# Splitting weight halves two halves ahead, and moving the form slots by 416 bytes

## The chip, the cores and the metric

The kernel runs on one NeuronCore of a Trainium2 chip. The metric is device time in microseconds (us). Three executions of the kernel before took 2930.47 us in the median (2928.84 to 2932.45).

The engines that matter here: TensorE (PE in the profile; its weight loads are listed as PEld), VectorE (DVE), ScalarE (ACT), GpSimd (POOL), and SyncE (SP), whose queue issues nearly all DMAs. Each engine runs its own instructions in the order in which the built program has them; semaphores make one engine wait for another. SBUF is the on-chip memory, with 128 partitions; an address below is a byte address within each partition. PSUM holds the results of matmuls in banks of 128x512 float32.

## The reference

One decoder layer in float32 for 512 tokens of width 2048. Two branches read the same normalised input: sliding-window attention and a gated delta rule over chunks of 64 tokens. Their outputs are gated, added, and projected once more.

```python
h = rms_norm(x, norm_w) * (1.0 + scale) + shift
proj = h @ w_in                      # 2048 x 21056
aq, ak, av, ag, d_qkv, dz, db, da, mg_a, mg_b = jnp.split(proj, ...)
a_out = swa_attention(aq, ak, av, sinks) * jax.nn.silu(ag)
y_a = a_out @ w_o_swa                # 2048 x 2048
d_qkv = causal_conv_silu(d_qkv, conv_w)
o = gated_delta_rule(dq, dk, dv, g, beta)
o = rms_norm(o, dn_norm_w) * jax.nn.silu(dz)
y_b = o @ w_o_dn                     # 4096 x 2048
y = jax.nn.sigmoid(mg_a) * y_a + jax.nn.sigmoid(mg_b) * y_b
return x + gate * (y @ w_out)        # 2048 x 2048
```

## The kernel before

**Products in three matmuls.** Weights and activations are float32, and each is split into a high part (a cast to the type fp32r) and a low part (the rest). A product is `wh*xh + wh*xl + wl*xh`, three matmuls (`mm3`, lines 265 to 267). `h` is kept split, as `hh` and `hl`. Weights come from DRAM in jobs of 1 MB (128x2048) and are split on the chip in halves of 128x1024: ACT casts (`whi`, line 68), DVE subtracts (`wlo`, line 69).

**Stages.** After the start-up (to about 120 us) come the delta rule's keys, attention, the delta rule's heads, and the closing chain (from about 1955 us). In the first three a job is one tile of 128 output channels (`channel_tile`): 16 pieces of the contraction, 8 in each half, three matmuls for each, so 24 matmuls in a half. The closing chain computes six 2048-wide products (the two gates `ga`, `gb`, the attention output, two halves of the delta output, the last projection) with a scheme of seven products for eight (`PRODUCTS`), on sums of quarters of the weights and of the activations. There a half holds 12 matmuls, and the activations are the stationary operand. The weight sums are made beside the earlier stages: `sums_of` loads quarters `q`, adds them on DVE (line 1490), and stores them to `s_d`. A solve (lines 819 and 827) runs on DVE beside the keys and the heads. In the heads a `scan` of four chunks runs for each of 16 groups; ACT and DVE copy and scale between its small matmuls (`vs`, line 972; `r`, line 960; `S`, lines 992 and 995).

**The weight line.** `jobs` lists all weights in the order of their use. Three counters run over it: `job_load` (loads written so far), `half_split` (halves split so far) and `half_used`. `half` hands out the half that a product needs, and splits it on the spot if that has not been written yet. When a product has been written with a half, `half_done` puts `split_half` on a list; at the next call of `pump` (after every second piece in a channel tile, after every half of tokens in the closing chain) `weight_tick` runs the list. `split_half` writes the cast and the subtraction of the next half, and after the second half of a job it puts `load_job` on the list for the pump after that, which writes the load of the job two later. So in the channel tiles, at the first pump of half n, the split of half n+1 is written.

**Buffers.** Raw weights have two buffers (`wraw`), and in the closing chain a third one (`oraw`, in the pool `braw`), which every third job uses from the 7th of the chain on; an extra `load_job` at the start of `tail` fills it first. Split halves have three buffers of `whi` and `wlo` (`whl`). A split needs its raw data landed and the third buffer free, that is, the product three halves before it done.

**Order.** The instructions are written by generators that `pump` steps beside the matmuls (`go`, `paced`, `beside`); `behind` ties an instruction to a place. A planner then settles each engine's order at build time: it runs the program with estimated durations, and an engine takes, of the instructions that are ready, the one written first. So the place in which an instruction is written is a priority, not a fixed position. DMAs on SP are ordered in the same way.

**Form slots.** The closing chain keeps the split activations in slots `f0` to `f8`, each a pair of 128x8x256 tiles of 8,192 bytes. Slots 5 to 8 take the place of `hh` and `hl` once these are done. Pools of the right side of SBUF are laid out downwards from its top: `work` (small tiles), `bf` (slots 2 to 4), `braw`, `bf01` (slots 0 and 1). In the built program `hh`, and later `f5h`, starts at 43,584, and all tiles of slots 5 to 8, `hh`, `hl`, `whi` and `wlo` start 64 bytes past a multiple of 512. The tiles of slots 0 to 4 start at 109,536 (`f0h`) to 191,456 (`f4l`), all of them 480 bytes past a multiple of 512. Between the end of `hl` (109,120) and `f0h` 416 bytes are unused.

Of the kernel before, what the change touches and what calls it, by code (L numbers as in the profile page):

```python
# [7 lines left out]
F32 = mybir.dt.float32  # L8
# [8 lines left out]
P = 128  # L17
# [35 lines left out]
class Layer:  # L53
# [148 lines left out]
    def load_job(self):  # L202
        j = self.job_load
        if j < len(self.jobs):
            src = self.jobs[j][1]
            third = j >= self.tail0 + 6 and (j - self.tail0) % 3 == 0
            pool, tag = (self.oraw, "rawo") if third else (self.wraw, "raw")
            raw = pool.tile([P, 2048], F32, tag=tag, name="raw")
            self.nc.sync.dma_start(out=raw[:, : src.shape[-1]], in_=src)
            self.raws[j] = raw  # L210
            self.job_load += 1
# [440 lines left out]
    def delta_keys(self):  # L652
        tc = self.tc
        dram = self.dram
        self.lt_d = dram.tile([2, 2, 16, 4, HD, HD], F32, name="lt_d")
        self.lab_d = dram.tile([VH, HD, 4, HD], F32, name="lab_d")
        self.ta_d = dram.tile([2, 16, 4, HD, HD], F32, name="ta_d")
        self.ts_d = dram.tile([2, 2, 16, 4, HD, HD], F32, name="ts_d")
        self.kT_d = dram.tile([KH, P, T], F32, name="kT_d")
        self.k_d = dram.tile([KH, P, T], F32, name="k_d")  # L660
        self.o_d = dram.tile([VH, P, T], F32, name="o_d")
        with ExitStack() as sa:
            self.ptp = sa.enter_context(tc.tile_pool(name="ptp", bufs=2, space=PSUM, reuse_waits="tile"))
            self.zpool = (sa.enter_context(tc.tile_pool(name="gwk", bufs=1, reuse_waits="tile")), "zth")
            wk = sa.enter_context(tc.tile_pool(name="dnA", bufs=2, reuse_waits="tile"))
            gp = sa.enter_context(tc.tile_pool(name="gates", bufs=1, reuse_waits="tile"))
            gates = self.gates(gp)
            self.go(gates, next(gates))
            gt = sa.enter_context(tc.tile_pool(name="gatew", bufs=1, reuse_waits="tile"))
            self.beside(self.gate(gt), 0.26, "gate")  # L670
            self.keys_done = []
            for g in range(NST):
                self.go(self.keys(wk, g, self.acc_k[g]), 10 + 8 * g)
            for h in ZAHEAD[:NFIRST]:
                self.z_tile(h)
            self.solved = []
            self.solves = self.paced(self.solve_all(), 0.36)
            ws = sa.enter_context(tc.tile_pool(name="wsumk", bufs=1, reuse_waits="tile"))
            sums = self.paced(self.weight_sums(ws, [0]), 1.7)
            for kind, j in self.mixed():  # L680
                if kind == "k":
                    self.go(self.keys(wk, j, self.channel_tile(f"k{j}")), 0)
                else:
                    self.z_tile(j)
            self.drain("gate")
            self.drain_slow(sums)
            self.drain_live()
# [391 lines left out]
    def tail(self, es, wk):  # L1079
# [4 lines left out]
        self.ys_d = self.dram.tile([5, P, 4, 256], F32, name="ys_d")  # L1084
        self.ya_d = self.dram.tile([4, 4, P, T], F32, name="ya_d")
        self.yo_d = self.dram.tile([4, 4, P, T], F32, name="yo_d")
        self.w = lambda name: wk.tile([P, T], F32, tag="w", name=name, bufs=2)
        self.ld = lambda name: wk.tile([P, T], F32, tag="ld", name=name, bufs=4)
        self.fo = lambda name: wk.tile([P, T], F32, tag="fo", name=name, bufs=4)
# [33 lines left out]
        for e, n, m in order:  # L1123
            name, form = PRODUCTS[m][:2]
# [757 lines left out]
```

## Time and profile before

| | before |
|---|---|
| median of 3 executions | 2930.47 us |
| the profiled execution, its own time | 2934.85 us |
| its span, from the first to the last instruction | 2933.1 us |
| mean granted clock of TensorE in it | 0.983 |
| PE busy | 2812.4 us (96%) |
| DVE busy | 2205.7 us (75%) |
| ACT busy | 1316.4 us (45%) |
| DMA, mean rate | 265 GB/s |

The profile is of one execution, taken by the hardware profiler. A row of waits reads: engine, tile and line that waited, what ended the wait, us in total, how often, the longest. A row of a group reads: line, engine, operation, out<-in, shapes, count, then busy us and mean ns of one, then idle us of the engine just before. Rows of stretches give the busy us of each engine with its instruction count, the granted clock of TensorE (1.00 is full speed), the busy share of the DMA engines and GB/s. Matmuls are pipelined: one is listed with about 0.39 us while the next starts 0.23 us after it.

### The profile page before, as it was taken

To read this page: it belongs to the slowest core of one execution; us is meant where nothing else is said; L and a number is where in the kernel's file an instruction comes from. 1 tells how busy PE (TensorE), PEld (TensorE's weight loads), DVE (VectorE), ACT (ScalarE), POOL (GpSimd) and SP (SyncE) were. 2 spreads that over 40 slices of the span, in tenths; PEclk is the share of its full clock that TensorE was granted. 3 is DMA by queue.
4 is the path that set the end of the run, shared out by engine and by line. 5 is a ranking of instruction groups with operands and counts; after the bars stand their busy time and mean duration, and the time that the engine had idled before them with its cause. 6 is when DMAs were issued, how large, how long until landed. Compare 5 with 4: busy or idle time off the path is not lost.

```text
span 2933.1 us, 38848 instructions
## 1 busy us (share of the span) xinstructions
PE 2812.4 (96%) x13864; PEld 2249.2 (77%) x13864; DVE 2205.7 (75%) x3422; ACT 1316.4 (45%) x2647; POOL 151.3 (5%) x124
## 2 busy tenths in 40 slices
PE   8999899899999999999997999999999999999999
PEld 6787677677776778878776777887878878778787
DVE  7876787778767768888865666768666878787876
ACT  5564433234454434344353434445444645444543
POOL 0001000000000001011000100100000000000000
PEclk9999999999999999999998999999999999999999
DMA  9889888464455548888868888866788989998875
GB/s 402 323 289 315 292 272 299 123 200 135 163 185 163 179 164 311 300 302 282 314 202 286 279 301 309 282 230 208 239 313 281 326 313 337 339 332 275 288 244 188
DMA packets 286565, 776.31 MB, mean 265 GB/s; under 512 B 82946, under 2 KB 107138, under 8 KB 241314
## 3 DMA queue, kind: packets, MB, share of 16 engines
q1 hardware_dynamic: 286372, 773.84, 76.7%
q8 instruction: 109, 1.79, 0.3%
q14 instruction: 84, 0.69, 0.1%
HBM read 588.84 MB, written 182.66 MB: 263 GB/s over the span
## 4 chain that ended last, share of the span: by engine, by line
PE 77%; DVE 10%; DMA 6%; ACT 3%; issue 3%; SPq 1%; POOL 0%; DVEq 0%; ACTq 0%; POOLq 0%
PE mm L267 13%; PE mm L265 13%; PE mm L266 13%; PE m L266 9%; PE m L267 9%; PE m L265 9%; DVE wlo L69 2%; DMA q<-in_w_q 1%; DMA s_d<-q 1%; DVE q L1490 1%; ACT whi L68 1%; PE pod L984 1%; PE pv L967 1%; PE O L1761 1%; PE pp L957 1%
## 5 line engine op out<-in xcount | busy, mean ns | idle before, releaser
L69 DVE TENSOR_TENSOR wlo<-raw,whi 128x1024 fp32r<-128x1024 f32 x588 | 722.7, 1235 | 327.8 <-ACT whi L68 326.2
L68 ACT CAST whi<-raw 128x1024 fp32r<-128x1024 f32 x588 | 612.4, 1050 | 697.6 <-PE m L267 400.2
L265 PE MATMUL mm<-hh,whi 128*128 128x512 f32 x2016 | 825.5, 409 | 24.7 <-ACT whi L68 24.3
L267 PE MATMUL mm<-hh,wlo 128*128 128x512 f32 x2016 | 803.9, 399 | 26.1 <-DVE wlo L69 26.0
L266 PE MATMUL mm<-hl,whi 128*128 128x512 f32 x2016 | 798.2, 396 | 0.0
L265 PEld LDWEIGHTS mm<-hh,whi 128*128 128x128 f32 x2016 | 384.4, 191 | 115.5 <-ACT whi L68 28.2
L267 PEld LDWEIGHTS mm<-hh,wlo 128*128 128x128 f32 x2016 | 383.6, 190 | 116.4 <-DVE wlo L69 34.4
L266 PEld LDWEIGHTS mm<-hl,whi 128*128 128x128 f32 x2016 | 384.4, 191 | 73.9 <-issue 1.5
L1490 DVE TENSOR_TENSOR q<-q,q 128x1024 f32<-128x1024 f32 (+1 forms) x224 | 244.3, 1091 | 16.3 <-DMA q<-in_w_q 14.9
L784 POOL TENSOR_SCALAR_AFFINE_SELECT E<-E 128x512 f32<-128x512 f32 x64 | 63.6, 1007 | 1048.1 <-DMA E<-g_rows 725.3
L827 DVE TENSOR_TENSOR A<-A,atmp 128x62 f32<-128x62 f32 (+30 forms) x124 | 110.0, 887 | 0.5
L819 DVE TENSOR_TENSOR atmp<-A 128x62 f32<-128x62 f32 (+30 forms) x124 | 108.6, 876 | 0.6
L642 DVE SCALAR_TENSOR_TENSOR yv<-mm,convh,yv 128x511 f32<-128x511 f32 (+2 forms) x96 | 71.4, 743 | 19.7 <-ACT yv L639 18.9
L790 ACT ACTIVATE E<-E,neg_g 128x128 f32<-128x128 f32 x256 | 79.2, 393 | 7.9 <-POOL E L784 7.8
L266 PE MATMUL m<-wlo,hh 128*128 128x512 f32 x192 | 76.9, 401 | 3.8 <-DVE wlo L69 3.8
L265 PE MATMUL m<-whi,hh 128*128 128x512 f32 x192 | 77.6, 406 | 2.0 <-ACT whi L68 1.8
L267 PE MATMUL m<-whi,hl 128*128 128x512 f32 x192 | 76.6, 400 | 0.0
L985 ACT COPY osb<-pod 128x256 f32<-128x256 f32 x64 | 23.8, 372 | 105.0 <-PE pod L984 80.2
L972 ACT ACTIVATE vs<-pv,kd 128x128 f32<-128x128 f32 x96 | 30.2, 365 | 81.0 <-PE pv L967 81.0
L266 PE MATMUL m<-wlo,f2h 128*128 128x512 f32 x160 | 63.7, 398 | 0.4 <-DVE wlo L69 0.4
L266 PE MATMUL m<-wlo,f0h 128*128 128x512 f32 x160 | 63.7, 398 | 0.0
L266 PE MATMUL m<-wlo,f3h 128*128 128x512 f32 x160 | 63.7, 398 | 0.0
(431 smaller groups left out, 4818.5 us busy)
## 6 DMA issues: line engine op xcount, KB each, us to landing
raw<-in_w_ch SPq DMA_DIRECT2D x126, 1024.0 KB
raw<-s_d SPq DMA_DIRECT2D x96, 1024.0 KB
q<-in_w_q SPq DMA_DIRECT2D x160, 512.0 KB
s_d<-q SPq DMA_DIRECT2D x160, 512.0 KB
raw<-in_w_q SPq DMA_DIRECT2D x72, 1024.0 KB
wa<-in_w_ada_ss SPq DMA_DIRECT2D x32, 1024.0 KB
gw<-in_w_ada_gate SPq DMA_DIRECT2D x16, 1024.0 KB
E<-g_rows SPq DMA_DIRECT2D x64, 256.0 KB
```

The costliest lines, as they stand in the source:

```text
L68: h = self.nc.scalar.copy(out=hi, in_=src)
L69: l = self.nc.vector.tensor_tensor(out=lo, in0=src, in1=hi.bitcast(F32), op=ALU.subtract)
L265: nc.tensor.matmul(ps, lhsT=wh, rhs=xh, start=first, stop=False)
L266: nc.tensor.matmul(ps, lhsT=wh, rhs=xl, start=False, stop=False)
L267: self.last_mm = nc.tensor.matmul(ps, lhsT=wl, rhs=xh, start=False, stop=last)
L642: nc.vector.scalar_tensor_tensor(out=y[:, s:], in0=ps[:, : T - s], scalar=w[:, j : j + 1], in1=y[:, s:], op0=ALU.mult, op1=ALU.add)
L784: self.last_mask = self.nc.gpsimd.affine_select(out=E, in_=E, pattern=[[0, NTB], [1, P]], compare_op=ALU.is_ge, fill=NEG, base=0, channel_ ...
L790: self.nc.scalar.activation(E[:, c, :], E[:, c, :], AF.Exp, bias=self.neg_g[:, c, h : h + 1])
L819: eng.tensor_tensor(out=t, in0=A[:, m : m + 1, m + 1 :].to_broadcast([P, m, n]), in1=A[:, :m, m : m + 1].to_broadcast([P, m, n]), op=ALU.mult,
L827: self.behind(eng.tensor_tensor(out=A[:, :m, m + 1 :], in0=A[:, :m, m + 1 :], in1=t, op=ALU.add))
L972: nc.scalar.activation(vs[:, e, :], pv[:, e, :], AF.Copy, scale=self.kd[:, c, 2 * g + e : 2 * g + e + 1])
L1490: self.behind(nc.vector.tensor_tensor(out=q[f], in0=q[x], in1=q[y], op=ALU.add))
```

## The change

Two splits more are put on the list once, at the start of the keys. Since every later split is put there by a `half_done`, the line of splits runs one half further ahead from then on: at the first pump of half n, the split of half n+2 is written, and each load of raw weights is written one half earlier too. The 7th load of the closing chain is then written in the heads, before the pool of the third raw buffer is opened; so the third buffer is used from the 10th job on. In the closing chain a tile of 104 float32 (416 bytes) is allocated first in the pool `work` and never used; what is allocated after it on the right side lies 416 bytes lower.

```diff
@@ load_job
-            third = j >= self.tail0 + 6 and (j - self.tail0) % 3 == 0
+            third = j >= self.tail0 + 9 and (j - self.tail0) % 3 == 0
             pool, tag = (self.oraw, "rawo") if third else (self.wraw, "raw")
@@ delta_keys
             self.beside(self.gate(gt), 0.26, "gate")
+            self.due += [self.split_half] * 2
             self.keys_done = []
@@ tail
         self.yo_d = self.dram.tile([4, 4, P, T], F32, name="yo_d")
+        wk.tile([P, 104], F32, name="align")
         self.w = lambda name: wk.tile([P, T], F32, tag="w", name=name, bufs=2)
```

## The prediction

> **What bounds the kernel now.** I read the shares of the engines first, then a table of five stages, then TensorE's waits stage by stage.
>
> ```profile
> span 2933.1 us, 38848 instructions
> PE 2812.4 (96%) x13864; PEld 2249.2 (77%) x13864; DVE 2205.7 (75%) x3422; ACT 1316.4 (45%) x2647; POOL 151.3 (5%) x124
> ...
> 120.00:550.00 430.00, 401.31 (x1845) 325.97 (x1843) 329.06 (x518) 185.05 (x463) 29.89 (x34) 0.97 0.84 281
> 550.00:1085.00 535.00, 524.31 (x2717) 396.07 (x2718) 411.96 (x833) 225.74 (x511) 34.03 (x22) 0.99 0.50 159
> 1085.00:1955.00 870.00, 825.08 (x4420) 673.87 (x4419) 647.91 (x993) 363.71 (x974) 87.18 (x64) 0.98 0.84 285
> 1955.00:2933.10 978.10, 956.77 (x4166) 774.36 (x4165) 722.16 (x940) 474.28 (x584) 0.00 (x0) 0.99 0.81 281
> ```
>
> TensorE is busy 2812.4 of 2933.1 us, so 121 us are idle; the stages are keys (from 120), attention (from 550), heads (from 1085) and closing chain (from 1955). The columns after the length are PE, PEld, DVE, ACT and POOL with their counts, then the granted clock, the DMA share and GB/s. No other engine is full in any stage: DVE is at 74 to 77%. So what counts is the idle time and the clock. The waits of TensorE, in the order keys, attention, heads, closing chain:
>
> ```profile
> PE mm L265 <- ACT whi L68: 9.2, 4, 5.0
> PE mm L267 <- DVE wlo L69: 7.0, 5, 3.7
> ...
> PE mm L267 <- DVE wlo L69: 2.9, 1, 2.9
> ...
> PE mm L267 <- DVE wlo L69: 16.2, 9, 6.0
> PE mm L265 <- ACT whi L68: 15.0, 9, 3.6
> PE pod L980 <- ACT vs L972: 5.2, 6, 1.7
> PE pp L957 <- DVE S L995: 3.0, 4, 1.9
> ...
> PE m L266 <- DVE wlo L69: 9.5, 7, 2.9
> PE m L265 <- ACT whi L68: 1.8, 1, 1.8
> ```
>
> Each row has the sum in us, the number, and the longest. Waits for a half of the weights make 9.2 + 7.0 + 2.9 + 16.2 + 15.0 = 50.3 us before 1955, and 11.3 us after it. None is over 6.0 us. A timeline around one of them, in the heads, shows why (columns: start, length, engine, line, operation, count, idle before):
>
> ```profile
> 1445.05 0.39 PE L266 MATMUL mm<-hl,whi 128*128 128x512 f32 x1
> 1449.64 0.80 PE L267 MATMUL mm<-hh,wlo 128*128 128x512 f32 x1 [4.20 <-DVE wlo L69]
> 1450.23 0.63 PE L265 MATMUL mm<-hh,whi 128*128 128x512 f32 x1
> ...
> 1443.39 1.98 ACT L68 CAST whi<-raw 128x1024 fp32r<-128x1024 f32 x2
> ...
> 1446.21 1.21 DVE L1490 TENSOR_TENSOR q<-q,q 128x1024 f32<-128x1024 f32 x1
> 1447.34 0.68 DVE L649 SCALAR_TENSOR_TENSOR yv<-th,yv 128x512 f32<-128x512 f32 x1
> 1447.95 0.50 DVE L819 TENSOR_TENSOR atmp<-A 128x342 f32<-128x342 f32 x1
> 1448.37 1.21 DVE L69 TENSOR_TENSOR wlo<-raw,whi 128x1024 fp32r<-128x1024 f32 x1
> ```
>
> The weights and their high part were there at 1445.4. The low part stood behind other work in DVE's order and came 4.2 us late, and after the stall the matmuls are 0.63 instead of 0.39 us long. The clock did that; here are the first, three of the middle and the sum of the 12 stretches of half clock that begin at such a wait between 120 and 1955:
>
> ```profile
> 277.43:280.84 3.41, 3.00 (x7) 2.42 (x8) 2.91 (x5) 3.17 (x11) 0.00 (x0) 0.50 0.96 197
> ...
> 1448.20:1455.02 6.82, 5.38 (x13) 3.85 (x14) 6.72 (x13) 0.63 (x1) 0.00 (x0) 0.50 0.98 338
> ...
> 1550.60:1564.25 13.65, 7.37 (x23) 5.88 (x24) 9.76 (x14) 4.09 (x11) 1.23 (x2) 0.50 0.78 277
> 1656.42:1659.82 3.40, 3.09 (x7) 2.50 (x8) 3.40 (x5) 0.52 (x2) 0.00 (x0) 0.50 0.00 0
> ...
> sum 64.75, PE 49.07 PEld 37.92 DVE 53.74 ACT 25.37 POOL 2.32; mean PE 4.09 PEld 3.16 DVE 4.48 ACT 2.11 POOL 0.19
> ```
>
> TensorE works 49.07 us in them at half speed, so half of that, 24.5 us, is lost. A wait for a half before 1955 thus costs half as much again: 50.3 + 24.5 = 74.8 us together.
>
> **Part one: the halves.** No instruction is added or removed; these two groups keep their counts.
>
> ```profile
> L69 DVE TENSOR_TENSOR wlo<-raw,whi 128x1024 fp32r<-128x1024 f32 x588 | 722.7, 1235 | 327.8 <-ACT whi L68 326.2
> L68 ACT CAST whi<-raw 128x1024 fp32r<-128x1024 f32 x588 | 612.4, 1050 | 697.6 <-PE m L267 400.2
> ```
>
> At the first pump of the keys two splits are written where there were none, 2 x 1.05 us on ACT and 2 x 1.24 on DVE; TensorE is then at half 16 with half 17 still to come, so nothing waits for them. From there on every split stands one half earlier in the written order. A half is 24 matmuls before 1955, at least 24 x 0.227 = 5.4 us (0.227 is 10.2/45 from the row of slot 8 below), and with other work between 870/110 = 7.9 us on average in the heads, which have 55 tiles of two halves. No wait is longer than that. So in the best case all 74.8 us go.
>
> Against that stand two things. First, the lateness is DVE's: from 1446.21 to 1449.6 it has no idle. Taken ahead, the subtraction makes everything that it passes 1.2 us later, and DVE is as far behind as before when TensorE comes to a product that cannot be prepared early: pod, pp, pv of the scan, which wait 5.2 + 3.0 us and some more now. Second, a half can be split only when its weights have landed, and only two raw buffers exist before 1955. The load of job j+2 is written at the pump after the second half of job j is split, so all loads move a half earlier too, past what SP issues in that time; SP already stands often at this place, for the subtraction that frees the buffer:
>
> ```profile
> SPq L209 <- DVE wlo L69: 593.5, 159, 11.6
> ...
> 583.76 0.38 SPq L209 DMA_DIRECT2D raw<-in_w_ch  x1
> ...
> 588.80 1.06 ACT L68 CAST whi<-raw 128x1024 fp32r<-128x1024 f32 x1 [3.14 <-DMA raw<-in_w_ch]
> ```
>
> A load alone takes 5.0 us (583.76 to 588.80), well inside the three halves that it has before and after. What it passes (stores s_d, loads q, E, qe, tt) is later once by one transfer, 5 us at most, since later loads pass no more than it did. DMA is at 84% in keys and heads, so the earlier place is worth something only if loads aren't already as late as the queue makes them. Bounds of the term: 0 and -74.8 us. I take 55%, -41 us: nearer the upper bound because every wait is shorter than the step, but not at it because DVE's lateness stays.
>
> In the closing chain the casts already run as early as a buffer allows:
>
> ```profile
> ACT whi L68 <- PE m L267: 370.2, 243, 3.4
> ...
> ACT whi L68 <- PE mm L266: 33.5, 12, 4.3
> ```
>
> From 2060 on 243 of some 300 casts wait for TensorE to let go of the third buffer (second row: in the heads 12 of 110). A place further ahead cannot make them earlier. Only the subtractions can win a place against other DVE work. Bounds 0 and -11.3; I take -3.
>
> **The third raw buffer** now starts with the 10th load of the chain instead of the 7th, as the 7th is written before that buffer exists. For three jobs the loads have two buffers: a job of two halves lasts 24 x 0.227 = 5.4 us there, and a buffer is held for the load (5.0) and two splits one half apart (2.7 + 1.05 + 1.24), 10.0 against 2 x 5.4. That fits; the cost is 0, and if a load is late by 2 us in each of the three, 6 us.
>
> **Part two: 416 bytes.** Slots 0 to 4 start at 480 bytes past a multiple of 512, slots 5 to 8 and both h tensors at 64 past one (given above). The tile of 416 bytes brings slots 0 to 4 to 64 as well. Their products differ today; 16 first matmuls of one product each:
>
> ```profile
> L265 PE MATMUL m<-whi,f8h x16: 389/389/389, 2895.0 to 2905.2; 128*128 128x512 f32 x16
> ...
> L265 PE MATMUL m<-whi,f3h x16: 394/394/394, 2905.9 to 2916.4; 128*128 128x512 f32 x16
> ...
> L265 PE MATMUL m<-whi,f0h 128*128 128x512 f32 x160 | 63.3, 396 | 0.0
> ...
> L265 PE MATMUL m<-whi,f4h 128*128 128x512 f32 x128 | 50.8, 398 | 0.0
> ```
>
> From the first to the 16th are 45 matmuls: 10.5 us for slot 3 and 10.2 for slot 8, so 0.3/45 = 6.7 ns each. Slots 0 to 3 have 160 such first matmuls each and slot 4 has 128: 768, times three is 2304 matmuls, times 6.7 ns is 15.4 us, all on TensorE, which is not waiting there. I take -15.4; the other bound is 0.
>
> [...] The rows show a difference between the two starts; I go by them.
>
> **Sum:** -41 - 3 + 0 - 15.4 = -59 against the profiled execution's 2934.85 us, which is 4.4 above the median of 2930.47: 2871 us by the median.
>
> **Rivals.** (a) All waits for halves go: -74.8 - 11.3 - 15.4, 2829 us. For it: no wait exceeds 6.0. Against it: DVE stays behind. (b) The two raw buffers are the limit: where a cast follows a landing, two ahead becomes one again, and only the slots and some 5 us remain: 2910. For it: 593.5 us of SP's waits and the 84%. Against it: at 1443 both halves were cast at once, so their data had been there. (c) The halves do as forecast, the slots' 6.7 ns come from something other than their start: 2886. (d) Slower: the cast now needs the buffer of the product that ends only as the position is reached; ACT and DVE stand at it, and the scan's copies vs and sums S queue behind, 1.05 + 1.24 us later. There are 48 such links (three in each of 16 groups), 110 us if all are hit, and TensorE waits for them. It turns the sign above 54% of the links (59/110); with three quarters hit, 2930 - 59 + 82 = 2953. Against it: in the heads only 12 of 110 casts wait for a buffer today, and the planner writes a split behind what is ready sooner. (e) No change by the noise: gains of (b) lost again in a new order, 2930.
>
> **How the numbers follow.** Forecast 0.42 (its own range 2850 to 2895), (a) 0.10, (b) 0.20, (c) 0.10, (d) 0.12, (e) 0.06. The range 2838 to 2932 leaves out most of (a) and (d). About 0.2% (6 us) is what a measurement can tell from no change: faster 0.82, same 0.06, slower 0.12.
>
> [...]
>
> **What would show it.** Right: the waits for whi and wlo before 1955 fall from 50 to under 20 us, stretches of half clock with them; slot 3 shows 389 ns and 10.2 us; the waits of pod, pp, pv and transposes rise a little. Wrong: casts ended by raw in number (b), slots still at 394 (c), or vs and S as TensorE's longest waits (d).

## The result

The changed kernel took 2912.14 us in the median of seven executions (2907.43 to 2922.3), the kernel before 2932.45 in the median of seven beside it. The ratio is 0.9935, with a 95% interval of 0.9919 to 0.9951: 19 us less, 14 to 24. The forecast was 2871, 59 less; its sign was right and its size was not.

**The profile after.** From the page, and from a table of three stretches: keys with attention, heads, closing chain. Here the borders are the first matmul of the heads' first tile and the first matmul of the chain, so that each kernel is cut at the same work. The columns are length, busy us of PE, PEld, DVE, ACT and POOL with their counts, granted clock, DMA share and GB/s. First the changed kernel:

```profile
span 2912.9 us, 38883 instructions
PE 2790.4 (96%) x13864; PEld 2243.9 (77%) x13864; DVE 2203.2 (76%) x3422; ACT 1319.0 (45%) x2647; POOL 158.2 (5%) x124
...
122.80:1090.90 968.10, 919.72 (x4540) 717.15 (x4539) 738.50 (x1345) 407.36 (x969) 62.93 (x56) 0.98 0.64 212
1090.90:1951.50 860.60, 822.94 (x4426) 672.54 (x4424) 644.98 (x990) 365.82 (x975) 95.05 (x64) 0.98 0.85 288
1951.50:2912.90 961.40, 939.52 (x4170) 772.44 (x4168) 722.77 (x944) 475.69 (x585) 0.00 (x0) 0.99 0.82 286
```

The kernel before, cut at the same matmuls:

```profile
122.90:1083.10 960.20, 920.82 (x4540) 718.10 (x4539) 737.85 (x1345) 406.97 (x969) 63.93 (x56) 0.98 0.65 214
1083.10:1954.30 871.20, 826.28 (x4426) 674.85 (x4424) 648.20 (x990) 364.48 (x975) 87.18 (x64) 0.98 0.84 285
1954.30:2933.10 978.80, 957.47 (x4171) 774.97 (x4168) 722.75 (x944) 474.98 (x585) 0.00 (x0) 0.99 0.81 281
```

The chain became 17.4 us shorter and the heads 10.6, but keys and attention 7.9 us longer. Up to the chain, where -41 was forecast, -2.8 remain (the start-up differs by 0.1). By these rows TensorE's idle time (length less PE) rose from 39.4 to 48.4 us in keys and attention and fell from 44.9 to 37.7 in the heads; its busy time fell by 4.4 us in the two together.

**The waits after.** TensorE's waits in the changed kernel, in the order keys, heads, closing chain (us in all, how often, the longest):

```profile
PE mm L267 <- DVE wlo L69: 9.4, 9, 2.4
PE mm L265 <- ACT whi L68: 6.4, 4, 2.6
PE pkk L757 <- ACT kT L750: 5.4, 7, 0.8
PE ptk L314 <- DVE y L649: 4.6, 1, 4.6
PE mm L265 <- DVE zth L307: 4.0, 2, 3.2
...
PE mm L267 <- DVE wlo L69: 12.2, 8, 2.8
PE mm L265 <- ACT whi L68: 7.8, 8, 1.8
PE pqk L919 <- DMA kT<-kT_d: 5.8, 1, 5.8
PE pto L314 <- DVE tt L936: 3.0, 3, 1.9
PE pv L968 <- DVE tt L936: 2.1, 3, 1.0
...
PE m L266 <- DVE wlo L69: 9.8, 8, 2.8
```

Before the chain the waits for halves are 9.4 + 6.4 + 12.2 + 7.8 = 35.8 us where they were 50.3, so 14.5 less. All other waits of TensorE there add up to 50 us where they were 34: kT, y and zth in the keys, one wait for the load of kT in the heads, the links tt of the scan. What the halves gave, other waits took, but not in the same stage. In keys and attention the waits for halves fell by 3.3 us only and the others rose by 12.2; in the heads they fell by 11.2 and the others rose by 3.9.

**The slots after.** Slot 3 at the same place as before (16 first matmuls, the times of the first and the last):

```profile
L265 PE MATMUL m<-whi,f3h x16: 389/389/389, 2884.7 to 2894.9; 128*128 128x512 f32 x16
```

10.2 us where it took 10.5, and 389 ns where it took 394, as forecast.

### The profile page after: what moved, and what is told of

It is laid out like the page before. It is cut to its first block, busy times and chain, and to the rows that moved or that the text cites. A ratio compares the mean times of both kernels' runs of the same rounds, so it can differ in the third digit from the quotient of the medians.

```text
span 2912.9 us, 38883 instructions
## 1 busy us (share of the span) xinstructions
PE 2790.4 (96%) x13864; PEld 2243.9 (77%) x13864; DVE 2203.2 (76%) x3422; ACT 1319.0 (45%) x2647; POOL 158.2 (5%) x124
## 4 chain that ended last, share of the span: by engine, by line
PE 74%; DVE 13%; DMA 6%; issue 3%; ACT 3%; SPq 1%; POOL 0%; DVEq 0%; ACTq 0%
PE mm L267 12%; PE mm L265 12%; PE mm L266 12%; PE m L266 9%; PE m L267 9%; PE m L265 9%; DVE wlo L69 3%; DMA raw<-in_w_ch 1%; DVE q L1492 1%; PE pv L968 1%; PE O L1763 1%; PE pod L985 1%; PE pp L958 1%; ACT sm L1731 1%; PE pod L984 1%
## 5 line engine op out<-in xcount | busy, mean ns | idle before, releaser
L265 PE MATMUL mm<-hh,whi 128*128 128x512 f32 x2016 | 821.2, 407 | 18.2 <-ACT whi L68 14.2
L265 PEld LDWEIGHTS mm<-hh,whi 128*128 128x128 f32 x2016 | 383.3, 190 | 107.9 <-ACT whi L68 17.8
L266 PEld LDWEIGHTS mm<-hl,whi 128*128 128x128 f32 x2016 | 383.3, 190 | 74.8 <-issue 2.0
L1492 DVE TENSOR_TENSOR q<-q,q 128x1024 f32<-128x1024 f32 (+1 forms) x224 | 247.9, 1107 | 14.5 <-DMA q<-in_w_q 13.2
L265 PE MATMUL m<-whi,hh 128*128 128x512 f32 x192 | 76.4, 399 | 0.2 <-DVE zth L307 0.2
L915 POOL TENSOR_TENSOR qe<-qe,yq 128x512 f32<-128x512 f32 x32 | 55.5, 1737 | 161.1 <-DMA qe<-eg_rows 149.5
```

The costliest lines, as they stand in the source:

```text
L265: nc.tensor.matmul(ps, lhsT=wh, rhs=xh, start=first, stop=False)
L266: nc.tensor.matmul(ps, lhsT=wh, rhs=xl, start=False, stop=False)
L915: self.behind(nc.gpsimd.tensor_tensor(out=qf, in0=qf, in1=q, op=ALU.mult), masks)
L1492: self.behind(nc.vector.tensor_tensor(out=q[f], in0=q[x], in1=q[y], op=ALU.add))
```

## The experiments

All ratios are to the kernel before, run beside each. "Heads" and "chain" below are lengths from the profiles, cut at the matmuls named above. A length is of one execution: in three runs whose chain is written as in the kernel before (before, e4, e10) the chain took 972.9 to 979.0 us.

### The two parts alone

e1 is the kernel before with the 416-byte tile alone; e2 is the changed kernel without it.

```diff
 # e1, against the kernel before
+        wk.tile([P, 104], F32, name="align")
 # e2, against the changed kernel
-        wk.tile([P, 104], F32, name="align")
```

> The kernel before with the 416-byte tile alone; the order of all instructions before the closing chain stays what it was. Theory one, that the slots' start addresses are worth what the intervals say and the halves are worth next to nothing: 15 us less than before, ratio 0.9948, with the first matmuls of slot 3 at 389 ns and a closing chain (first of its matmuls to the end) of 963 to 965 us against 978.8. Rival, that the gain of the changed kernel comes from the halves and the slots hardly count: within 6 us of before, slot 3 at 394 ns.

> The changed kernel without the 416-byte tile: splits one half further ahead and the third buffer from the 10th load. Theory one: 3 to 6 us less than before, ratio 0.998 to 0.999; waits for split halves between 120 and 1955 us at about 36 us as in the changed kernel, other waits of TensorE there at about 50 instead of 34. Rival, that both parts gain and disturb each other when they are together: 15 us or more less than before. My forecast of the prediction for this part alone was 44 less.

e1: 2915.25, ratio 0.9939 (0.9922 to 0.9956), 18 us less, with slot 3 at 389 ns. e2: 2927.79, ratio 0.9977 (0.9965 to 0.9989), 3 to 10 us less. Keys and attention, heads and chain are 970.7, 860.2 and 974.1 us long in e2 and 958.7, 868.9 and 967.1 in e1: the pattern of longer keys and shorter heads belongs to the halves. Within their intervals the parts add up, and most of the gain is the slots'.

### Is the load late on SP?

In the heads a load of weights was issued 11.7 us after its raw buffer came free (12.8 before), in part behind stores of weight sums that wait for VectorE. e3 and e4 take that wait away, in the changed kernel and in the one before.

```diff
-            self.behind(nc.sync.dma_start(out=dst[n, f, i][:, cols], in_=q[f]))
+            self.behind(nc.sync.dma_start(out=dst[n, f, i][:, cols],
+                                          in_=q[f] if self.fixed is None else self.fixed))
 # delta_heads
+            self.fixed = ws.tile([P, 1024], F32, name="fixed")
+            nc.gpsimd.memset(self.fixed, 0.01)
```

> The changed kernel, but in the heads each store of a weight sum writes a fixed tile instead of the sum, so SP no longer stands at these stores for VectorE's additions (same bytes stored, same additions made, but the closing chain computes with fixed numbers for the sums of four of its six products). Theory S, that in the heads a load of weights is late because SP stands ahead of it at a store: the load is issued under 6 us after its buffer is free instead of 11.7, the waits of TensorE for split halves in the heads fall from 20 us to under 8, and the time falls by 12 us or more against the changed kernel. Theory A, that casts and subtractions are late in the orders of ACT and DVE whatever SP does: loads are issued earlier, but 14 us or more of these waits stay and the time moves by less than 5 us.

> The kernel before with the same fixed tile in the stores of the heads (the closing chain computes with fixed numbers for the sums of four of its six products). Theory S: waits for split halves in the heads fall from 31 us to under 15 and the time by 15 us or more. Theory A: they stay above 22 and the time moves by less than 8 us. Together with the kernel that has both, this shows whether the step of one half is worth more when SP is not in the way: by S the difference between the two in the heads grows beyond the 10 us of now or both lose nearly all waits; by A it stays.

e3: 2912.55, ratio 0.9931 (0.9912 to 0.9949), the same as the changed kernel. e4: 2929.47, ratio 0.9988 (0.9978 to 0.9998), some 3 us below the kernel before. In both the sums of four of the chain's six products are left out and replaced by a fixed tile. The loads did come earlier: in the mean 6.1 us after the buffer came free instead of 11.7. The waits of TensorE for halves in the heads did not follow: 19.9 us against 20.0, and 28.7 in e4 against 31.2. From the timelines of ACT, SP and TensorE at one late half, first the changed kernel:

```profile
1343.34 0.50 SPq L209 DMA_DIRECT2D raw<-in_w_ch  x1
...
1359.35 0.69 ACT L639 ACTIVATE yv<-mm,convh 128x512 f32<-128x512 f32 x1 [4.22 <-PE mm L267]
1359.94 1.98 ACT L68 CAST whi<-raw 128x1024 fp32r<-128x1024 f32 x2
...
1361.02 0.50 PE L265 MATMUL mm<-hh,whi 128*128 128x512 f32 x1 [0.89 <-ACT whi L68]
1364.11 0.80 PE L267 MATMUL mm<-hh,wlo 128*128 128x512 f32 x1 [2.35 <-DVE wlo L69]
```

and e3 at the same half:

```profile
1337.37 0.33 SPq L209 DMA_DIRECT2D raw<-in_w_ch  x1
...
1354.07 0.69 ACT L640 ACTIVATE yv<-mm,convh 128x512 f32<-128x512 f32 x1 [4.22 <-PE mm L267]
1354.66 1.98 ACT L68 CAST whi<-raw 128x1024 fp32r<-128x1024 f32 x2
...
1355.74 0.50 PE L265 MATMUL mm<-hh,whi 128*128 128x512 f32 x1 [0.89 <-ACT whi L68]
1358.83 0.79 PE L267 MATMUL mm<-hh,wlo 128*128 128x512 f32 x1 [2.35 <-DVE wlo L69]
```

In both the cast stands in ACT's order right behind the reading of the previous tile's product (yv), and that reading waits for TensorE's last matmul of the tile. So the cast cannot begin before TensorE is through with its work, though ACT is idle for 4.22 us before and the load was issued 17 us earlier. TensorE then waits 0.89 us for the cast and 2.35 us for the subtraction, to the hundredth the same in both kernels. Theory S fell.

### Is VectorE behind?

e9 and e10 leave the 128 additions of the sums out of the heads; e11 moves them to GpSimd.

```diff
 # e9, e10, in the heads only
-            self.behind(nc.vector.tensor_tensor(out=q[f], in0=q[x], in1=q[y], op=ALU.add))
 # e11, in the heads only
-            self.behind(nc.vector.tensor_tensor(out=q[f], in0=q[x], in1=q[y], op=ALU.add))
+            self.behind(nc.gpsimd.tensor_tensor(out=q[f], in0=q[x], in1=q[y], op=ALU.add))
```

> The changed kernel without the 128 additions of the weight sums in the heads (quarters are loaded and stored as they are, so four of the six products of the closing chain compute with single quarters in place of sums); 128 x 1.11 us = 142 us less work for VectorE there, and no store waits for VectorE. In the built order of ACT the casts of the heads stand where they stand in the changed kernel (2.2 places ahead of the kernel before instead of 2.6). Theory D, that TensorE's waits in the heads come from VectorE running behind: its waits there for halves (20 us) and for the scan and conv links (18 us) fall together to under 15 us, and the time falls by 20 us or more. Theory O, that the order fixed at build time holds the casts behind results of TensorE itself: the waits for whi stay near 8 us and the time falls by less than 10 us.

> The kernel before without the same 128 additions (four of the six products of the closing chain compute with single quarters in place of sums). Theory D: the waits for halves in the heads fall from 31 us to under 12 and the time by 25 us or more, and of the step of one half nothing is left to gain in the heads. Theory O: whi keeps 12 us or more of its 15 us, the time falls by less than 12 us.

> The changed kernel with the 128 additions of the weight sums in the heads on GpSimd instead of VectorE; nothing is left out. GpSimd's additions are not in the traces at this size; 1.74 us for 128x512 gives some 3.5 us each, 445 us in a stage of 870 in which GpSimd is busy for 95 us. Theory D: 10 to 25 us less than the changed kernel, if VectorE's other instructions keep their durations. Rival: the two engines slow each other (VectorE's 128x1024 subtraction above 1.4 us instead of 1.23) or GpSimd's queue makes the sums late, and the time rises.

e9: 2901.39, ratio 0.9901 (0.9886 to 0.9916), some 10 us below the changed kernel. e10: 2921.91, ratio 0.9965 (0.9951 to 0.9979), 10 us below the kernel before. The waits for halves in the heads, of e9 and then of e10:

```profile
PE mm L267 <- DVE wlo L69: 9.0, 9, 2.4
PE mm L265 <- ACT whi L68: 7.8, 8, 1.8
```

```profile
PE mm L265 <- ACT whi L68: 15.0, 7, 7.4
...
PE mm L267 <- DVE wlo L69: 2.8, 5, 1.0
```

The waits for whi, 7.8 us in eight, are the same in the changed kernel, e2, e3 and e9, and they sum to 15.0 us in the kernel before and, in other pieces, in e10: neither SP nor VectorE changes their sum. That is theory O, with a gain at the edge of what it allows. VectorE's load decides only the rest: without the additions wlo falls from 16.2 to 2.8 us in the kernel before, and from 12.2 to 9.0 in the changed one. With 149 us less work on VectorE (645.0 to 496.0 us busy in the heads) the gain is 10 us, below the 20 or more of theory D.

e11 took 3004.46, ratio 1.0257 (1.0233 to 1.0282). In its heads an addition on GpSimd takes 2.69 us, and VectorE's subtraction became 1.70 us long; the last row is the subtraction in the changed kernel's heads (all three rows are from 1085 to 1952 us).

```profile
L1494 POOL TENSOR_TENSOR q<-q,q 128x1024 f32<-128x1024 f32 x121 | 326.0, 2694 | 399.1 <-DMA q<-in_w_q 371.6 <-issue 16.7 <-DMA qe<-eg_rows 4.0
L69 DVE TENSOR_TENSOR wlo<-raw,whi 128x1024 fp32r<-128x1024 f32 x101 | 169.9, 1700 | 55.4 <-ACT whi L68 54.4 <-DMA s_d<-q 0.6
```

```profile
L69 DVE TENSOR_TENSOR wlo<-raw,whi 128x1024 fp32r<-128x1024 f32 x111 | 138.2, 1260 | 47.2 <-ACT whi L68 46.9
```

So the rival was right on VectorE: beside GpSimd's additions its subtraction, which reads two tiles in SBUF, took 1.70 us against 1.26, while the convolution's instructions, which read one input from PSUM, kept their 0.744 us. Whether GpSimd was slowed too is not shown.

### What if the halves really come early?

e5 and e6 give every load of weights and every split high priority with the planner, in the changed kernel and in the one before; f1 does it in the heads alone; f2 besides writes the load of kT earlier, and f3 does only that.

```diff
 # weight_tick: e5, e6 up to the heads' end; f1, f2 in the heads alone
         for f in due:
-            f()
+            with self.tc.high_priority():
+                f()
 # queries: f2, f3
+        kT = wk.tile([P, T], F32, tag="kT", name="kT")
+        nc.sync.dma_start(out=kT, in_=self.kT_d[g])
         yield from self.conv(wk, ps, g, q)
         M = [self.decay_load(wk, 2 * g + e) for e in range(2)]
-        kT = wk.tile([P, T], F32, tag="kT", name="kT")
-        nc.sync.dma_start(out=kT, in_=self.kT_d[g])
```

> The changed kernel, with every load of weights and every split that the list of pump writes put at the planner's high priority up to the heads' end. In the built order of ACT the first half of a job in the heads is cast 19.5 places earlier than in the kernel before (the change as it is: 2.6 places; a half is about 9 places long). Theory P, that the splits are late because the planner places the loads, and with them the casts, behind other work: the waits for split halves between 120 and 1955 us fall from 36 us to under 10, and if nothing takes their place the time falls by 15 to 35 us against the changed kernel. Rival d, that ACT and VectorE are so full that splits made earlier only push the scan's links back: the waits for halves fall, but other waits of TensorE rise by as much, and the time stays within 6 us or rises.

> The kernel before (one half ahead, slots where they were), with the same high priority for loads and splits. In the built order the casts of the heads stand where they stand in the changed kernel with that priority. If the place on SP is all that matters, as in theory P, this gains as much against the kernel before as the other gains against the changed one and 4 to 6 us more, since the step of a half is then worth nothing: 20 to 40 us less than before. If the step of a half counts in itself, waits for halves stay clearly above those of the other kernel, by 10 us or more.

> The changed kernel with loads of weights and splits at high priority in the heads alone, so that start-up, keys and attention stay as they are in the changed kernel. In the built order the casts of the heads stand 16.9 places (first halves) and 12.1 places (second halves) earlier than in the changed kernel. Theory Z, that in the heads a wait removed from the halves comes back elsewhere: waits for halves in the heads under 3 us instead of 20, but waits for kT, for the conv's sums (yq, yv) and for lab together at 25 us or more, the heads 5 to 20 us longer than the changed kernel's 860.6, and the time 5 to 20 us above the changed kernel. Rival, that the 92 us of the kernel with the priority everywhere came from start-up and keys and the heads gain: 5 us or more below the changed kernel.

> The same, and the load of kT is written ahead of the convolution of q instead of behind it (two to six places earlier on SP). Theory Z, with the passed loads as its largest term: the waits for kT (17 us in the kernel with the priority everywhere) fall under 4 and the time falls by 8 to 20 us against the kernel without this edit. Rival, that kT is late because VectorE and ACT hold the links and not because its load is: kT's wait goes over to yq or S, and the time stays within 4 us.

> The changed kernel with only the load of kT written ahead of the convolution of q; the places of all casts and weight loads stay the same. If the changed kernel's one wait for kT (5.8 us at 1555, with 10.2 us of half clock in which TensorE works 7.75 us) is a price of loads that were passed: the wait goes and 4 to 10 us with it, 2903 to 2909. If the jam at that place only changes its name (the kernel before has 9.6 us of waits for a half at 1551 to 1558): another wait of 4 us or more stands between 1545 and 1575 and the time stays within 3 us.

e5: 3003.86, ratio 1.0254 (1.0234 to 1.0274). e6: 3017.94, ratio 1.0303 (1.0289 to 1.0317). So theory P was right on the waits for halves (0.9 us are left up to the chain in e5) and wrong on the time. Against the changed kernel e5 lost 21 us in the start-up, 42 in keys and attention, where the weight loads now pass all others, and 27 behind them; f1 leaves the first two out. f1: 2936.8, ratio 1.002 (1.0009 to 1.0031), some 25 us above the changed kernel, with heads of 873.2 us against 860.6. f2: 2932.62, ratio 1.0001 (0.9989 to 1.0013), 4 to 6 us below f1, between theory Z and its rival. f3: 2914.18, ratio 0.994 (0.9924 to 0.9955), no change against the changed kernel.

The heads of f1, in the columns of the tables above:

```profile
1094.10:1967.30 873.20, 818.31 (x4348) 661.37 (x4347) 644.35 (x972) 362.40 (x947) 78.47 (x60) 0.97 0.84 279
```

They hold 78 matmuls fewer than the heads of the other kernels (x4348, not x4426): small ones of the last scans, which come behind the chain's first matmul here. So the length that can be compared is that of heads and chain together: 1843.9 us in f1, 1822.0 in the changed kernel, 1836.0 in e1, which has the same slots without the step. TensorE's waits in the heads of f1 (its lines are 4 to 8 higher; L269 is L265 there):

```profile
PE pqk L926 <- DMA kT<-kT_d: 17.3, 8, 9.3
PE mm L269 <- DVE yq L647: 13.3, 3, 6.2
PE py L934 <- DMA lab<-lab_d: 7.2, 5, 2.5
PE mm L269 <- DVE yv L647: 6.2, 3, 2.9
...
PE mm L269 <- ACT whi L68: 1.9, 2, 0.9
```

and of f2:

```profile
PE mm L269 <- DVE yv L647: 14.4, 5, 4.3
PE py L934 <- DMA lab<-lab_d: 13.8, 11, 3.9
PE mm L269 <- DVE yq L647: 10.5, 4, 4.4
PE pqk L926 <- DMA kT<-kT_d: 6.5, 6, 3.1
```

In f1 the waits for halves are gone, 1.9 us of 20.0, and the casts run the moment their buffer is free, as ACT's own waits show (of the changed kernel, then of f1: idle time of ACT ahead of its casts in the heads):

```profile
L68 ACT CAST whi<-raw 128x1024 fp32r<-128x1024 f32 x111 | 114.2, 1052 | 46.5 <-PE mm L266 45.1 <-DMA raw<-in_w_ch 0.8
```

```profile
L68 ACT CAST whi<-raw 128x1024 fp32r<-128x1024 f32 x110 | 115.5, 1050 | 196.8 <-PE mm L270 196.2
```

In their place stand 44 us for what the loads and splits were moved past: the loads of kT and lab on SP, and the convolution's sums on VectorE, without which a product's PSUM bank is not free (the waits of mm for yq and yv, 13.3 + 6.2 us). That is theory Z. All waits of TensorE in the heads but those for halves are 52.9 us in f1, 17.5 in the changed kernel. With kT's load written earlier (f2), 10.8 us leave kT, and lab and yv take 14.8 more; in f3 the wait for kT stays at 5.2 us. f1's forecast of 5 to 20 us was a little low. e6 shows the same from the other side: with the priority, its casts stand where e5's do, so the step of one half is worth nothing, and its distance of 14 us to e5 is near what the slots give. Its forecast of a gain of 20 to 40 us was wrong.

### The step only where it gained

```diff
 # delta_keys
-            self.due += [self.split_half] * 2
 # delta_heads
+            self.due += [self.split_half]
```

> The changed kernel, but the line of splits is moved one half further ahead at the start of the heads instead of the start of the keys: keys and attention keep the orders of the kernel before, heads and closing chain those of the changed kernel. In three kernels with the early step keys and attention took 965 to 971 us, in two without it 958 to 960, and the heads 860 with it and 869 to 871 without. If these differences are of the order and not of the single executions: keys and attention 958 to 961, heads 859 to 862, closing chain 961, and the time 5 to 9 us below the changed kernel, near 2905. If they are of the executions alone, it stays within 3 us of the changed kernel's 2912 to 2914.

f5: 2906.42, ratio 0.9915 (0.9901 to 0.9929), the lowest of all kernels that compute everything. Its keys and attention are as before, its heads and chain as in the changed kernel:

```profile
123.10:1079.80 956.70, 918.85 (x4539) 717.25 (x4538) 737.48 (x1346) 406.59 (x969) 62.81 (x56) 0.98 0.65 215
1079.80:1939.30 859.50, 823.29 (x4426) 673.54 (x4424) 646.25 (x990) 365.91 (x975) 85.92 (x64) 0.98 0.84 288
1939.30:2898.50 959.20, 938.93 (x4171) 771.14 (x4168) 722.01 (x944) 474.87 (x585) 0.00 (x0) 1.00 0.82 287
```

The loss in keys and attention therefore belongs to the early step there: in eight kernels that have it they take 964.7 to 970.9 us, in five without it 956.7 to 960.2. The interval overlaps that of the changed kernel (0.9919 to 0.9951), and the two were not run beside each other, so the 6 us between them, as forecast, rest on the profiles as much as on the times.

### Which start is good?

e7 and e8 put tiles of 32 and 64 bytes in place of the 416; e12 gives each slot another start; f4 moves the weights, h and slots 5 to 8 by 64 bytes.

```diff
 # e7: [P, 8]   e8: [P, 16]   e12: [P, 24], and 64 bytes after slots 0 to 3   f4: [P, 40]
-        wk.tile([P, 104], F32, name="align")
+        wk.tile([P, 8], F32, name="align")
 # f4, first in the pool const
+            self.const.tile([P, 16], F32, name="shift")
```

> The changed kernel with a tile of 32 bytes in place of 416: slots 0 to 4 start 448 bytes past a multiple of 512, which is 0 past a multiple of 64 (and 64 past one of 128, as slots 5 to 8). If what counts is the start against 64 bytes: slot 3 shows 389 ns and 10.2 us from the first to the 16th, as with 416 bytes, and the closing chain is as long as the changed kernel's 961 us within 4. If 128 or 512 bytes past the same place counts for more than 64: not told apart here for 128, but for 512 slot 3 would show 394 ns and 10.5 us and the chain 976 or more.

> The changed kernel with a tile of 64 bytes in place of 416: slots 0 to 4 start 416 bytes past a multiple of 512, which is 32 past a multiple of 64, as in the kernel before. If the start against 64 bytes counts: slot 3 shows 394 ns and 10.5 us again, and the closing chain is 13 us or more longer than the changed kernel's 961. If any move off the old place is enough (which tiles lie beside each other, not the start): 389 ns and 961.

> The changed kernel with the slots at five different starts: slots 4, 3, 2, 1, 0 begin 384, 320, 256, 192 and 128 bytes past a multiple of 512 (tiles of 96 bytes first and 64 bytes between). So far from one matmul to the next: 227 ns at 64 past, 231 to 234 at 416, 448 and 480 past. If the nearness to the end of a block of 512 bytes costs, the intervals fall step by step from 384 to 128; if only the one start at 64 is good (the start of the weight halves, which are read at the same time), all five stay at 231 to 234; if multiples of 128 or 256 are good, slots 0, 2, 4 or slot 2 alone show 227.

> The changed kernel with 64 bytes ahead of everything on the left side and a tile of 160 bytes in place of 416: whi, wlo, hh, hl and slots 5 to 8 start 128 bytes past a multiple of 256, slots 0 to 4 stay at 64 past one. In the closing chain a slot is the stationary operand and a weight half the moving one, in the heads the other way round. If the stationary operand's own start counts: slots 0 to 4 stay at 227 ns from matmul to matmul, slots 5 to 8 go to 234, and the heads, whose stationary whi and wlo moved, get longer by some 2640 x 7 ns = 18 us. If the two operands have to start alike: slots 5 to 8 and the heads stay at 227 ns and slots 0 to 4 go to 231 or more. If the moving operand's start counts: all slots go up together.

One execution each took 2927.31 us (e7), 2924.13 (e8), 2922.84 (e12) and 2923.1 (f4); what counts here are the intervals between matmuls. 16 first matmuls of one product, with the times of the first and the last (45 steps apart). e7 and e8, slot 3:

```profile
L265 PE MATMUL m<-whi,f3h x16: 390/393/404, 2898.4 to 2908.9; 128*128 128x512 f32 x16
```

```profile
L265 PE MATMUL m<-whi,f3h x16: 392/397/400, 2895.1 to 2905.6; 128*128 128x512 f32 x16
```

e12, slots 4, 3, 2 and 1:

```profile
L265 PE MATMUL m<-whi,f4h x16: 393/396/398, 2828.5 to 2839.0; 128*128 128x512 f32 x16
...
L265 PE MATMUL m<-whi,f3h x16: 389/389/389, 2894.2 to 2904.4; 128*128 128x512 f32 x16
...
L265 PE MATMUL m<-whi,f2h x16: 388/388/398, 2839.7 to 2850.0; 128*128 128x512 f32 x16
...
L265 PE MATMUL m<-whi,f1h x16: 390/392/404, 2483.2 to 2493.7; 128*128 128x512 f32 x16
```

f4, slots 3 and 8:

```profile
L265 PE MATMUL m<-whi,f3h x16: 392/392/392, 2894.6 to 2904.9; 128*128 128x512 f32 x16
...
L265 PE MATMUL m<-whi,f8h x16: 389/389/389, 2883.7 to 2893.9; 128*128 128x512 f32 x16
```

A start on a multiple of 64 is not enough (e7: 10.5 us, against my expectation), nor is 64 past a multiple of 128. In e12 slot 3 alone, 256 bytes from the start of the weights, shows 10.2 us, which none of the three forecasts had. In f4 slot 8 starts at 128 past a multiple of 256 and keeps 10.2 us, because the weights start there too; slot 3 stays at 64 and needs 10.3. So it is not the slot's own start that counts but its distance from the start of the weight half in the same matmul, modulo 256 bytes. That is the forecast of f4 by which the two have to start alike, though slots 0 to 4 came out nearer, at 228.9 ns and not 231 or more. By the median length of a half of 12 matmuls in six kernels:

| slot start minus weight start, modulo 256 | from matmul to matmul | seen in |
|---|---|---|
| 0 | 226.7 ns | changed kernel, slots 5 to 8 of all, slot 3 of e12 |
| 64 | 233.3 | slots 0 and 4 of e12 |
| 96 | 234.3 | e8 |
| 128 | 232.6 to 232.8 | e7, slot 1 of e12 |
| 160 | 233.3 | the kernel before |
| 192 | 228.9 | slot 2 of e12, slots 0 to 4 of f4 |

Distances 0, 64 and 128 were each reached as they stand and 256 bytes further on (slots 3 and 4 of e12, and e7), and 192 with two starts of the weights (f4, slot 2 of e12), each time with the same result within 0.2 ns. Why the distance counts is not shown; only these six distances were tried.

## Why the prediction failed where it did

**The 416 bytes: right.** 2304 matmuls x 6.7 ns = 15.4 us was the term; the halves of slots 0 to 4 went from 2.80 to 2.72 us, the chain from 978.8 to 967.1 in e1 and 961.4 in the changed kernel, and e1 gave 18 us (13 to 23). What I had right was the price; the reason I could not name is the distance from the weights. Rival (c), that something other than the start makes the 6.7 ns, fell in e1, where nothing but the start changed.

**The halves before the chain: the step that failed.** It is the term of -41 us, taken "nearer the upper bound because every wait is shorter than the step". The step was a half in the written order, which I took for a half in ACT's order. Counted in the order of ACT's instructions, the casts of first halves in the heads moved by 2.6 places and those of second halves by 1.8, where a half is 790/110 = 7.2 places long (the trace lists 974 entries of ACT in the heads of the kernel before; 184 of them are readings of an accumulator and no places in this count; the 9 places in the expectation of e5 include them). In keys and attention, by the same count, the casts moved by 0.7 places in the mean, and 109 of 142 did not move ahead at all. The written order is only a priority among what the planner holds to be ready. A cast is not ready before its load, and the planner places that behind other transfers: with loads and splits raised together the casts of first halves moved 17 to 20 places; with the splits alone raised, in a program that was built but not run, they stand 2.7 places ahead, as without it.

So the waits for halves before the chain fell by 14.5 us and not by some 28 of 50 plus their clock, and other waits rose by 16. That second number is what the sum put at nothing: the prediction said that pod, pp and pv would wait "some more", and gave it no price. A smaller misreading is in the bound of 74.8 us: of the twelve stretches of half clock the one at 294.50 begins behind waits for kT and y (3.1 us from 290.4 on) and not behind a wait for a half; it is 2.4 of the 24.5 us. In f1, where the waits for halves in the heads vanish as in rival (a), heads and chain together take 7.9 us more than in e1, with the same slots, by one profile of each. Which passed instruction caused each of the new waits in keys and attention was not tested; f5 shows only that they come with the early step.

**"DVE's lateness stays"** was named as the reason against the upper bound, and it is a part only: without 128 of VectorE's additions the sum of the waits for whi stays (7.8 and 15.0 us), those for wlo fall.

**Rivals (b) and (d).** The measured 2912 is the number of (b), 2910, but not its mechanism: in the changed kernel casts in the heads wait 0.8 us for a landing, and 5.6 us of earlier loads (e3) change nothing. The mechanism of (d), links pushed back by splits, is there, but with other places than I priced: not vs and S, but in the keys kT, y and zth, in the heads tt and the loads that were passed (kT, in f1 lab too), and in f1 the convolution's sums that free a PSUM bank. In keys and attention of the changed kernel it takes more than the halves give, in its heads less (3.9 us against 11.2); with the halves forced early (f1) it outweighs the gain in the heads too.

**The chain and the third buffer: not contradicted.** The chain of e2, which holds the halves and the buffer's later start without the slots, is 4.7 us shorter than before (974.1 against 978.8), where -3 and 0 were taken. The same chain varies by 6 us from one execution to another (972.9 in e4, 979.0 in e10), so the size is not shown; a cost of the buffer of 6 us or more does not show either.

**The signs in the profile** told which term had failed: 35.8 us of waits for whi and wlo before the chain, where under 20 were to be left, while slot 3 came out as announced, at 389 ns and 10.2 us. The stretches of half clock before the chain fell too, from 82 to 65 us. None of the three signs of being wrong came: not casts ended by raw, not slots at 394, not vs and S as the longest waits.

## What to carry to other kernels

Where a planner settles the order, moving an instruction in the written order is no measure of how much earlier it runs: count its place in the engine's own order, before and after, and look at what stands directly ahead of it. A wait that is removed from one operand is worth something only if the next operand of the same stage is early; price what the moved loads pass, by name, before taking any share of the waits as a gain. And make an early step only in the stage where it gains: the heads won 11 us by it, keys and attention lost 8.

## What the runs showed of the hardware

In these runs the interval between the chain's matmuls went with the distance between the starts of the two operands, modulo 256 bytes (table above): 226.7 ns at a distance of 0, 2 to 8 ns more at the five others. With both starts moved by 64 bytes together (f4, slot 8) it stayed as it was, 10.2 us for 45 steps. In e11 an addition of 128x1024 float32 on GpSimd, beside VectorE's work, took 2.69 us, and beside it VectorE's subtraction of two SBUF tiles took 1.70 instead of 1.26 us. Moving these additions (without them VectorE is busy 149 us less in the heads, e9) to GpSimd, which was busy for 95 of 867 us there, cost 92 us against the changed kernel.
